# Preparing the DeltaNet chunks of a hybrid diffusion layer: loads, convolution, beta and the copies' engine

## The chip, the cores and the metric

The kernel runs on one core of a Trainium2 chip. The metric is the time of one execution on the device in microseconds (us). A core has five engines with an instruction queue each: TensorE (PE, with its weight loads as PEld) for matrix products, VectorE (DVE), ScalarE (ACT), GpSimd (POOL), and SyncE (SP), which here issues most of the transfers (DMAs). Matrix products write to PSUM, of which this kernel uses banks of 128 x 512 floats; everything else works on SBUF tiles of 128 partitions. Tensors that are too large for SBUF go through DRAM.

## The reference, cut to what matters

One layer works on 1024 latent tokens and 256 context tokens of width 1024. A modulated, RMS-normalised input is projected once; one half of the columns feeds a gated DeltaNet (4 heads of 128), the other a 2-D neighbourhood attention (8 heads of 64). Both are concatenated, projected, added to the input, and a SwiGLU feed-forward layer follows. The part that the change touches is the DeltaNet:

```python
qkv = short_conv(p[..., :3 * DN_WIDTH], conv_w)      # depthwise, 5 taps, centred, then SiLU
...
gam = cumsum(g)                                       # within a chunk
decay = exp(where(tril, gam[..., :, None] - gam[..., None, :], -inf))
kb = k * beta[..., None]
m = where(strict, einsum("bhncd,bhnmd->bhncm", kb, k) * decay, 0.0)
a_mat = eye(CHUNK) + m
u = triangular_solve(a_mat, v * beta[..., None], ...)
w = triangular_solve(a_mat, kb * exp(gam)[..., None], ...)
qk = where(tril, einsum("bhncd,bhnmd->bhncm", q, k) * decay, 0.0)
```

Both directions (forward, and backward over the flipped sequence) are scanned, the context first. The chunk's length does not alter the result, and the kernel uses chunks of 128.

## The kernel before, in words

**Stages.** (1) Norms, modulation and the first two blocks of the projection. (2) The rest of the projection as a list of `jobs` (lines 953 to 962), with the chunks' preparation beside it. (3) The scans over the chunks, with the neighbourhood attention beside them. (4) The output projection, and the feed-forward layer. The change lies in stage 2.

**Jobs.** A `Block` computes 128 output columns for all tokens, transposed: for each of eight slices of the input width, products of the high and low parts of weights and input (`mm_part`, line 390; matmuls at line 395). Kinds q, k and v are convolved along the tokens, nq and nk are the attention's. A `Wide` job computes 256 or 264 columns with the tokens on the partitions, tile by tile of 128 tokens (`wide`, line 573; matmuls at line 578): z, the output gate, goes to `z_d`, and nv, the attention's values, to `nv_d`. Each tile is copied from PSUM by ScalarE into `zt` (two buffers) and stored by a DMA that ScalarE's queue issues (lines 589 and 604). Weights pass a raw buffer of which there is one; ScalarE makes the high part (lines 197 and 570), GpSimd the low part (lines 198 and 571).

**A block's end.** `evac` copies the block from PSUM to `cr` (line 443) and issues all of the convolution to VectorE at once: a multiplication (line 447) and four multiply-adds (line 451), each in a context and a latent part. `silu` (line 458) follows on ScalarE at the end of the same job. `norm` is run in the next job, and `finish` in the one after: it makes the transposed copies and the products k k^T (`kk_d`) and q k^T (`qk_d`). After the second nv job, sixteen DMAs copy windows of `nv_d` into `vw_d` (line 1024). The main loop (lines 975 to 1028) takes a step of the background after each slice or tile: one to five generator steps.

**The background.** `block_inverses` solves the 32 x 32 diagonal blocks of `a_mat` for all 40 chunk-heads and both directions on VectorE (lines 824 and 826). The results `U` and their transposes `ut` (line 844) go to `x_d` (lines 845 and 846). `preps` then prepares 20 chunks: two directions times two context and eight latent chunks. The latent ones start when all q blocks are finished. At most three chunks are live, each takes one step in a round, and one further chunk may be loaded (`landing`, line 936).

**One chunk (`prep`, line 879).** `fetch` loads `kk` (k k^T, four heads), `xc` (the inverses of its blocks, both ways) and, for latent chunks, `at` (q k^T). Step 1: GpSimd multiplies the high and low parts of the log decays with a triangular mask into `rg` (line 886, 128 x 512 twice); ScalarE copies four diagonal blocks into `fx` (line 891), GpSimd four into `x0` (line 892). Step 2: TensorE sums the log decays (lines 896 and 897), ScalarE takes the exponential `e` (line 900), VectorE forms kk = kk * (-beta) * e, head by head since -beta differs (line 902; `NB` is minus beta over the squared norm of k), and am = at * e (line 906). Step 3: TensorE multiplies kk with fx (line 911), ScalarE copies the result (line 913). Steps 4 to 6: three products with the running sum, each followed by an addition on VectorE (lines 920 and 921). `y` is stored to `y_d`, `am` to `at_d`, by SP (line 930).

**What sets the order.** Every engine has one queue, worked off in order. The order within a queue is made when the program is built: a planner takes the instructions by priority, which is the program's order, as they become ready by its own cost estimates. So an instruction can stand ahead of one that was written before it; the sixteen copies of line 1024 stand between loads of the preparation on SP. A tile with n buffers can be written again when the tile n before it has been read. All DMAs share eight semaphores (100, 102 to 108 in the trace) in rotation, and a queue that issues one waits until the transfer that had the semaphore before has landed, whoever issued it.

Of the kernel before, what the change touches and what calls it, by code (L numbers as in the profile page):

```python
# [87 lines left out]
def hybrid(ctx, tc, a, dbg):  # L88
# [278 lines left out]
    with ExitStack() as bs:  # L367
# [30 lines left out]
        class Block:  # L398


            def __init__(self, kind, i):
                self.kind, self.i = kind, i
                self.segs = SEGS[1:] if kind in ("q", "nq") else SEGS
                self.t0 = self.segs[0][0]
# [16 lines left out]
            def evac(self):  # L421
# [22 lines left out]
                for lo, hi in ((0, CT), (CT, T)):  # L444
                    if hi <= t0:
                        continue
                    dve.tensor_scalar(acc[:, lo:hi], raw[:, lo:hi], cw[:, blk, 2:3], None, op0=OP.mult)
                    for tap in (0, 1, 3, 4):
                        o = tap - 2
                        d0, d1 = max(lo, lo - o), min(hi, hi - o)  # L450
                        dve.scalar_tensor_tensor(acc[:, d0:d1], raw[:, d0 + o:d1 + o],  # L451
                                                 cw[:, blk, tap:tap + 1], acc[:, d0:d1],
                                                 op0=OP.mult, op1=OP.add)

# [99 lines left out]
        class Wide:  # L554
# [27 lines left out]
            def tiles(self):  # L582
                half = self.half
                if self.kind == "nv":
                    for t in range(NCH):
                        p = self.wide(t, 0, 256)
                        vt = cp.tile([128, 264], F32, name="zt", tag="zt", bufs=2)
                        act.copy(vt[:, :256], p[:, :256])
                        act.dma_start(nv_d[t * 128:(t + 1) * 128, half * 256:half * 256 + 256], vt[:, :256])
                        yield  # L590
                    return
# [6 lines left out]
                for t in range(2, NCH):  # L598
                    p = self.wide(t, 0, 264)
                    zt = cp.tile([128, 264], F32, name="zt", tag="zt", bufs=2)  # L600
# [3 lines left out]
                    act.dma_start(z_d[(t - 2) * 128:(t - 1) * 128, half * 264:half * 264 + nz], zt[:, :nz])  # L604
                    yield

# [157 lines left out]
        def block_inverses():  # L764
            with ExitStack() as gs:
# [75 lines left out]
                for d in range(2):  # L841
                    ud = U[:, d * NU:(d + 1) * NU]
                    ut = g4.tile([128, NU, 32], F32, name="ut", tag="ut")
                    dve.transpose(fl(ut), fl(ud))
                    sp.dma_start(x_d[:, d, d], ud)
# [7 lines left out]
        def preps():  # L853

            first_half.close()
            with ExitStack() as gs:
# [11 lines left out]
                def fetch(d, c):  # L868

                    kk, xc = work("kk", 4), pp.tile([128, 2, 4, 32], F32, name="xc", tag="xc", bufs=2)  # L870
# [3 lines left out]
                    if c >= 2:  # L874
                        at = work("at", 2)
                        sp.dma_start(at, qk_d[:, c - 2])
                    return d, c, kk, xc, at

                def prep(n, d, c, kk, xc, at):
                    lat = c >= 2  # L880
                    mle = M[C_LE + d].rearrange("p (o i) -> p o i", o=1).to_broadcast([128, 4, 128])
                    rgs = []
                    for gg in (GH, GL):
                        rg = work("rg", 2, F32R)
                        src = gg.bitcast(F32)[:, d, c].rearrange("p (h o) -> p h o", o=1).to_broadcast([128, 4, 128])
                        pool.tensor_tensor(rg, src, mle, OP.mult)
                        rgs.append(rg)
                    x0, fx = x0s[n % 3], fxs[n % 2]
                    for b in range(4):
                        q = slice(b * 32, b * 32 + 32)  # L890
                        act.copy(fx[q, :, q], xc[q, 1])
                        pool.tensor_copy(x0[q, :, q], xc[q, 0])
# [6 lines left out]
                    e = work("y", 4)  # L899
                    act.activation(fl(e), p, AF.Exp)  # L900
                    for h in range(4):
                        dve.scalar_tensor_tensor(kk[:, h], kk[:, h], NB[:, d, c, h:h + 1], e[:, h],
                                                 op0=OP.mult, op1=OP.mult)
# [31 lines left out]
                while live or todo or landing:  # L935
                    if not landing and todo and (todo[0][1] < 2 or all(x in done for x in queries)):
# [38 lines left out]
        for n in range(2, len(jobs) + 2):  # L975
# [17 lines left out]
            nrm = blk(n - 1)  # L993
            if isinstance(j, Wide):
                for t, _ in enumerate(j.tiles()):
                    next(fin, 0)
                    if t == 4 and nrm:
                        nrm.norm()
# [10 lines left out]
            elif j:  # L1009
                for k in range(KT):  # L1010
                    j.mm([k])
                    if k >= 3:
                        next(fin, 0)
# [11 lines left out]
            if nrm:  # L1025
                nrm.norm()
            if isinstance(j, Block):
# [645 lines left out]
```

## Time and profile before

| | |
|---|---|
| median of 3 runs | 1618.23 us (1617.94 to 1624.84) |
| profiled execution | 1618.78 us, its span 1617.0 us |
| TensorE busy | 1512.7 us (94%) |
| VectorE, ScalarE, GpSimd busy | 1039.2, 706.2, 210.8 us |
| granted TensorE clock over the span | 0.979 |

The span runs from the first to the last instruction of the program. In the profile's lines, L911 is line 911; `out<-in` names the tiles; "x8" counts instructions; ACTq and SPq are an engine's queue issuing a DMA or waiting. A wait is idle time of an engine before an instruction, put down to whatever ended last before it. `issue` means that the profile shows nothing that was waited for. Stage 2 ends about 640 us into the span; the chunks' preparation runs from about 296 to 602 us, the four context chunks until about 337 us and the latent ones from 423 us on.

### The profile page before, as it was taken

Reading aid. Unit: us, or ns where it says so; the run is one execution under the profiler, and the core shown is the slowest. Engines: PE = TensorE matmul, PEld = TensorE weight load, DVE = VectorE, ACT = ScalarE, POOL = GpSimd, SP = SyncE. Lnnn points to the kernel's source line nnn. Section 1 sums busy time; section 2 is a strip of 40 time slices with the busy share of each in tenths; the row PEclk is TensorE's granted clock in tenths of the full one; section 3 lists DMA queues with packets and bytes.
Section 4 is the critical chain, followed back from the end, with each engine's and each line's share of the span. In section 5 each row is a group of like instructions: output and inputs, shape, how many; then the busy total and the mean of one; then the engine's idle time right before and its main releaser. Section 6 shows DMA issues by size and latency. Waiting matters only on the chain.

```text
span 1617.0 us, 24090 instructions
## 1 busy us (share of the span) xinstructions
PE 1512.7 (94%) x8642; PEld 1275.1 (79%) x8642; DVE 1039.2 (64%) x1931; ACT 706.2 (44%) x1341; POOL 210.8 (13%) x279
## 2 busy tenths in 40 slices
PE   2899899999989798999898999999999999999999
PEld 1689787778888786888787787888888888888887
DVE  4785678445264467577898638966656656679652
ACT  5353363663332234666674337433333333444441
POOL 0144611422232320111110000000000000000000
PEclk9898999999999899999999999999999999999999
DMA  9267121545346528999853910532223333698742
GB/s 370 89 209 218 56 76 40 177 129 173 120 126 194 185 95 212 312 282 283 234 178 119 324 46 33 196 105 98 98 98 110 101 109 113 231 365 307 253 157 85
DMA packets 206407, 271.03 MB, mean 168 GB/s; under 512 B 15952, under 2 KB 115792, under 8 KB 205264
## 3 DMA queue, kind: packets, MB, share of 16 engines
q1 hardware_dynamic: 200240, 264.14, 50.2%
q10 hardware_dynamic: 6048, 5.35, 1.0%
q8 instruction: 68, 1.11, 0.3%
q14 instruction: 51, 0.42, 0.1%
HBM read 204.68 MB, written 68.94 MB: 169 GB/s over the span
## 4 chain that ended last, share of the span: by engine, by line
PE 76%; DVE 10%; ACT 5%; DMA 4%; issue 2%; POOL 1%; SPq 0%; ACTq 0%; DVEq 0%; POOLq 0%
PE ps L1249 26%; PE ps L1592 13%; PE blk L395 11%; PE blk L578 4%; PE pr L920 3%; PE ps L1376 3%; PE sc L316 2%; PE sc L306 2%; PE sc L294 2%; DVE N L826 1%; DMA at<-qk_d 1%; DMA wad<-wa 1%; DVE tt L824 1%; DVE cacc L451 1%; PE pr L911 1%
## 5 line engine op out<-in xcount | busy, mean ns | idle before, releaser
L395 PE MATMUL blk<-hh,whi 128*128 128x512 f32 (+1 forms) x416 | 123.9, 390 | 1.4 <-ACT hh L690 1.0
L1310 ACT CAST uhi<-wq 128x512 fp32r<-128x512 f32 x101 | 60.4, 621 | 140.7 <-issue 61.6
L395 PE MATMUL blk<-hl,whi 128*128 128x512 f32 (+1 forms) x416 | 117.1, 374 | 5.0 <-DVE hl L692 5.0
L1310 ACT CAST uhi<-ws 128x512 fp32r<-128x512 f32 x91 | 54.7, 622 | 152.9 <-PE ps L1249 74.2
L395 PE MATMUL blk<-hh,wlo 128*128 128x512 f32 (+1 forms) x416 | 117.7, 375 | 0.6 <-POOL wlo L198 0.6
L1311 DVE TENSOR_TENSOR ulo<-wq,uhi 128x512 fp32r<-128x512 f32 x101 | 67.1, 686 | 69.0 <-ACT uhi L1310 38.9
L1249 PE MATMUL ps<-hT,uhi 128*128 128x512 f32 x336 | 104.0, 391 | 3.1 <-ACT hT L1424 3.1
L1249 PE MATMUL ps<-hT,ulo 128*128 128x512 f32 x336 | 103.9, 390 | 0.0
L1249 PE MATMUL ps<-lT,uhi 128*128 128x512 f32 x336 | 103.9, 391 | 0.0
L578 PE MATMUL blk<-zhi,hh 128*128 128x256 f32 (+2 forms) x304 | 90.1, 296 | 0.0
L1249 PE MATMUL ps<-hB,uhi 128*128 128x512 f32 x288 | 89.3, 391 | 0.0
L1249 PE MATMUL ps<-lB,uhi 128*128 128x512 f32 x288 | 89.2, 391 | 0.0
L395 PEld LDWEIGHTS blk<-hl,whi 128*128 128x128 f32 x416 | 73.7, 192 | 19.6 <-DVE hl L692 5.3
L1249 PE MATMUL ps<-hB,ulo 128*128 128x512 f32 x288 | 89.1, 390 | 0.0
L578 PE MATMUL blk<-zhi,hl 128*128 128x256 f32 (+2 forms) x304 | 88.4, 291 | 0.0
L578 PE MATMUL blk<-zlo,hh 128*128 128x256 f32 (+2 forms) x304 | 87.7, 289 | 0.0
L395 PEld LDWEIGHTS blk<-hh,wlo 128*128 128x128 f32 x416 | 73.3, 191 | 16.0 <-issue 1.6
L1311 DVE TENSOR_TENSOR ulo<-ws,uhi 128x512 fp32r<-128x512 f32 x91 | 60.7, 685 | 37.8 <-ACT uhi L1310 29.4
L395 PEld LDWEIGHTS blk<-hh,whi 128*128 128x128 f32 x416 | 71.3, 193 | 15.2 <-issue 3.6
L1249 PEld LDWEIGHTS ps<-hT,uhi 128*128 128x128 f32 x336 | 63.1, 189 | 16.5 <-ACT hT L1424 3.5
L1249 PEld LDWEIGHTS ps<-lT,uhi 128*128 128x128 f32 x336 | 63.4, 189 | 13.3
L1249 PEld LDWEIGHTS ps<-hT,ulo 128*128 128x128 f32 x336 | 63.3, 189 | 13.2
(341 smaller groups left out, 3719.5 us busy)
## 6 DMA issues: line engine op xcount, KB each, us to landing
wq<-w_fo SPq DMA_DIRECT2D x99, 256.0 KB
wq<-w_gu SPq DMA_DIRECT2D x88, 256.0 KB
wad<-wa SPq DMA_DIRECT2D x64, 256.0 KB
bt<-rpb SPq DMA_DIRECT2D x64, 192.0 KB
t_d<-g SPq DMA_DIRECT2D x22, 512.0 KB
fr<-t_d SPq DMA_DIRECT2D x44, 256.0 KB
f_d<-g SPq DMA_DIRECT2D x33, 256.0 KB
fr<-f_d SPq DMA_DIRECT2D x33, 256.0 KB
```

The source lines that it names most:

```text
L294: pe.matmul(sc[:, u * 640 + n0:u * 640 + n1], q, ks[i], start=i == 0, stop=i == 1)
L306: pe.transpose(sc[:, u * 640 + j * 128:u * 640 + (j + 1) * 128], bt[:, j * 128:(j + 1) * 128], ident)
L316: pe.matmul(sc[u * ND:u * ND + ND, 1280:1408], vv, pt[:, j * 128:(j + 1) * 128], start=j == 0, stop=j == 4)
L395: pe.matmul(o, ww[:, k], xx[k][:, s], start=k == 0 and j == 0, stop=k == KT - 1 and j == 2)
L451: dve.scalar_tensor_tensor(acc[:, d0:d1], raw[:, d0 + o:d1 + o], cw[:, blk, tap:tap + 1], acc[:, d0:d1], op0=OP.mult, op1=OP.add)
L578: pe.matmul(p[:, :c1 - c0], x[k][:, s], ww[:, k, c0:c1], start=k == 0 and j == 0, stop=k == KT - 1 and j == 2)
L920: pe.matmul(p[:, hs[h]], f[:, h], src[:, h], start=True, stop=True)
L1249: pe.matmul(o, w[wi][:, k], x[xi][:, k], start=first and k == 0 and j == 0, stop=k == n - 1 and j == 2, skip_group_check=True)
L1310: act.copy(hi, self.raw[key])
L1311: dve.tensor_tensor(lo, self.raw[key], hi.bitcast(F32), OP.subtract)
L1376: pe.matmul(o, w[wi][:, k], parts[xi][k][:, s], start=k == 0 and j == 0, stop=k == KT - 1 and j == 2)
L1592: pe.matmul(o[b], w[wi][:, b], F[xn, p][xi], start=n in (0, 1, 5) and p == 0 and j == 0, stop=p == NFB // 2 - 1 and j == 2, skip_group_che ...
```

## The change

Six edits in stage 2:

- A block's convolution becomes a generator: the multiplication, then one tap at a time for both parts. The next job takes one step of it per slice or tile. `silu` runs at its end, and not at the end of the block's own job.
- The DMAs that store nv and z tiles are issued by SP, one tile later (`held`); `zt` has three buffers.
- Minus beta is multiplied into the inverses that go to `fx`, once per direction, before they are stored in `x_d`. In a chunk, the four products of line 902 become one.
- Up to two chunks may be loaded ahead; `kk` has five buffers in place of four, `xc` and `at` three in place of two.
- `rg` is made by ScalarE, eight instructions of 128 x 128 in place of two of 128 x 512 on GpSimd, in four buffers in place of two. `x0` is filled by ScalarE too.
- `y` has five buffers in place of four.

```diff
@@ Block
-                for lo, hi in ((0, CT), (CT, T)):
-                    if hi <= t0:
-                        continue
+                self.taps = self.conv(raw, blk)
+
+            def conv(self, raw, blk):
+
+                acc = self.acc
+                parts = [(lo, hi) for lo, hi in ((0, CT), (CT, T)) if hi > self.t0]
+                for lo, hi in parts:
                     dve.tensor_scalar(acc[:, lo:hi], raw[:, lo:hi], cw[:, blk, 2:3], None, op0=OP.mult)
-                    for tap in (0, 1, 3, 4):
-                        o = tap - 2
+                yield
+                for tap in (0, 1, 3, 4):
+                    o = tap - 2
+                    for lo, hi in parts:
                         d0, d1 = max(lo, lo - o), min(hi, hi - o)
                         dve.scalar_tensor_tensor(acc[:, d0:d1], raw[:, d0 + o:d1 + o],
                                                  cw[:, blk, tap:tap + 1], acc[:, d0:d1],
                                                  op0=OP.mult, op1=OP.add)
+                    yield
+                self.silu()
@@ Wide.tiles (nv; z alike)
                         p = self.wide(t, 0, 256)
-                        vt = cp.tile([128, 264], F32, name="zt", tag="zt", bufs=2)
+                        if held:
+                            sp.dma_start(*held.pop())
+                        vt = cp.tile([128, 264], F32, name="zt", tag="zt", bufs=3)
                         act.copy(vt[:, :256], p[:, :256])
-                        act.dma_start(nv_d[t * 128:(t + 1) * 128, half * 256:half * 256 + 256], vt[:, :256])
+                        held.append((nv_d[t * 128:(t + 1) * 128, half * 256:half * 256 + 256], vt[:, :256]))
                         yield
+                    sp.dma_start(*held.pop())
@@ block_inverses
                     dve.transpose(fl(ut), fl(ud))
+                    x = (ut, ud)[d]
+                    dve.tensor_tensor(x, x, NB[:, d].rearrange("p c (h o) -> p (c h) o", o=1).to_broadcast(
+                        [128, NU, 32]), OP.mult)
                     sp.dma_start(x_d[:, d, d], ud)
                     sp.dma_start(x_d[:, d, 1 - d], ut)
@@ preps
-                    kk, xc = work("kk", 4), pp.tile([128, 2, 4, 32], F32, name="xc", tag="xc", bufs=2)
+                    kk, xc = work("kk", 5), pp.tile([128, 2, 4, 32], F32, name="xc", tag="xc", bufs=3)
...
-                        at = work("at", 2)
+                        at = work("at", 3)
...
-                    mle = M[C_LE + d].rearrange("p (o i) -> p o i", o=1).to_broadcast([128, 4, 128])
                     for gg in (GH, GL):
-                        rg = work("rg", 2, F32R)
-                        src = gg.bitcast(F32)[:, d, c].rearrange("p (h o) -> p h o", o=1).to_broadcast([128, 4, 128])
-                        pool.tensor_tensor(rg, src, mle, OP.mult)
+                        rg = work("rg", 4, F32R)
+                        for h in range(4):
+                            act.activation(rg[:, h], M[C_LE + d], AF.Copy, scale=gg.bitcast(F32)[:, d, c, h:h + 1])
...
                         act.copy(fx[q, :, q], xc[q, 1])
-                        pool.tensor_copy(x0[q, :, q], xc[q, 0])
+                        act.copy(x0[q, :, q], xc[q, 0])
...
-                    e = work("y", 4)
+                    e = work("y", 5)
                     act.activation(fl(e), p, AF.Exp)
-                    for h in range(4):
-                        dve.scalar_tensor_tensor(kk[:, h], kk[:, h], NB[:, d, c, h:h + 1], e[:, h],
-                                                 op0=OP.mult, op1=OP.mult)
+                    dve.tensor_tensor(kk, kk, e, OP.mult)
...
-                    if not landing and todo and (todo[0][1] < 2 or all(x in done for x in queries)):
+                    while len(landing) < 2 and todo and (todo[0][1] < 2 or all(x in done for x in queries)):
                         landing.append(fetch(*todo.pop(0)))
@@ main loop
+            taps = nrm.taps if nrm and nrm.taps else iter(())
             if isinstance(j, Wide):
                 for t, _ in enumerate(j.tiles()):
                     next(fin, 0)
+                    next(taps, 0)
                     if t == 4 and nrm:
+                        for _ in taps:
+                            pass
                         nrm.norm()
...
             elif j:
                 for k in range(KT):
                     j.mm([k])
+                    next(taps, 0)
...
             if nrm:
+                for _ in taps:
+                    pass
                 nrm.norm()
-            if isinstance(j, Block):
+            if isinstance(j, Block) and not j.taps:
                 j.silu()
```

More of the change, by code (lines that the diff above doesn't have):

```diff
@@ L402, in __init__ @@
                 self.kind, self.i = kind, i
+                self.taps = None
                 self.segs = SEGS[1:] if kind in ("q", "nq") else SEGS
@@ L583, in tiles @@
                 half = self.half
+                held = []
                 if self.kind == "nv":
@@ L599, in tiles @@
                     p = self.wide(t, 0, 264)
-                    zt = cp.tile([128, 264], F32, name="zt", tag="zt", bufs=2)
+                    if held:
+                        sp.dma_start(*held.pop())
+                    zt = cp.tile([128, 264], F32, name="zt", tag="zt", bufs=3)
                     act.activation(zt[:, :nz], p[:, :nz], AF.Silu)
@@ L603, in tiles @@
                         act.copy(ab[:, t], p[:, 248:264])
-                    act.dma_start(z_d[(t - 2) * 128:(t - 1) * 128, half * 264:half * 264 + nz], zt[:, :nz])
+                    held.append((z_d[(t - 2) * 128:(t - 1) * 128, half * 264:half * 264 + nz], zt[:, :nz]))
                     yield
+                sp.dma_start(*held.pop())
         first = [Block("k", 0), Block("k", 1)]
```

## The prediction

> **What bounds the kernel now.** I read the page first, then the stages in windows, then who ended TensorE's waits inside them, and last the chain and the single queues around each long wait.
>
> ```profile
> span 1617.0 us, 24090 instructions
> PE 1512.7 (94%) x8642; PEld 1275.1 (79%) x8642; DVE 1039.2 (64%) x1931; ACT 706.2 (44%) x1341; POOL 210.8 (13%) x279
> ```
>
> TensorE is busy 94%, and the change removes no matmul. So only its idle time, and the time it runs at a lowered clock, can be won. The windows (stretch, its length, busy time of PE, PEld, DVE, ACT and POOL, granted clock, DMA share, GB/s) cover the chunks' preparation:
>
> ```profile
> 285.00:345.00 60.00, 55.53 (x278) 43.74 (x277) 27.39 (x38) 36.85 (x62) 27.09 (x45) 0.97 0.47 153
> 345.00:425.00 80.00, 79.69 (x510) 71.63 (x509) 34.25 (x41) 32.38 (x46) 13.16 (x5) 0.98 0.46 148
> 425.00:520.00 95.00, 84.26 (x588) 77.56 (x587) 53.44 (x82) 33.50 (x73) 37.54 (x54) 0.95 0.49 152
> 520.00:608.00 88.00, 78.64 (x488) 69.40 (x487) 46.91 (x73) 24.93 (x49) 24.75 (x38) 0.94 0.45 146
> ```
>
> The first holds the four context chunks, the last two the sixteen latent ones. Idle in these two: 95 - 84.26 + 88 - 78.64 = 20.1 us. Lost to the clock: 0.05 x 95 + 0.06 x 88 = 10.0 us. The first adds 4.5 us idle and 0.03 x 60 = 1.8 us of clock. The ceiling of the whole change is the sum, 36.4 us, or 2.2%. The 80 us of the q blocks hold 0.3 us idle: nothing to win there. Who ended TensorE's waits, in 425 to 608 us and (second fence) 285 to 345 us (total, times, longest):
>
> ```profile
> PE pr L911 <- DVE y L921: 6.2, 3, 4.3
> PE pr L911 <- issue: 5.2, 2, 3.1
> PE pr L920 <- ACT kk L913: 4.3, 2, 3.1
> PE pr L911 <- DVE kk L902: 3.5, 6, 0.9
> ```
>
> ```profile
> PE pr L896 <- POOL rg L886: 2.0, 3, 1.3
> PE pr L911 <- DVE kk L902: 1.1, 2, 0.6
> ```
>
> The five longest, in TensorE's timeline (start, length, what, and in brackets the idle time before it):
>
> ```profile
> 449.08 1.16 PE L911 MATMUL pr<-fx,kk 128*128 128x128 f32 x8 [1.65 <-DVE y L921]
> ...
> 468.01 1.60 PE L911 MATMUL pr<-fx,kk 128*128 128x128 f32 x8 [2.07 <-issue]
> ...
> 506.53 2.07 PE L920 MATMUL pr<-y,kk 128*128 128x128 f32 x8 [3.11 <-ACT kk L913]
> ...
> 530.74 2.04 PE L911 MATMUL pr<-fx,kk 128*128 128x128 f32 x8 [3.12 <-issue]
> ...
> 547.54 2.07 PE L911 MATMUL pr<-fx,kk 128*128 128x128 f32 x8 [4.33 <-DVE y L921]
> ```
>
> The eight small matmuls behind the last three take about 2.05 us where those at 449 took 1.16: the lowered clock follows the wait. What stood behind 506 (chain of waits: start, length) and 530 (ScalarE's timeline), and, last line, behind 547:
>
> ```profile
> 491.70 4.25 DMA nv_d<-zt
> ...
> 497.51 7.88 DMA at<-qk_d
> ...
> 505.47 0.33 ACTq L589
> ...
> 505.89 0.59 ACT kk L913
> ```
>
> ```profile
> 525.36 0.33 ACTq L589 DMA_DIRECT2D nv_d<-zt  x1
> ...
> 528.42 0.33 ACTq L589 DMA_DIRECT2D nv_d<-zt  x1
> 528.79 0.60 ACT L900 ACTIVATE y<-pr 128x512 f32<-128x512 f32 x1 [2.64 <-DMA y_d<-y]
> ```
>
> ```profile
> 533.90 12.21 DMA at<-qk_d
> ```
>
> Twice ScalarE's queue stood at its own store of a value tile (L589), which could be issued only when an unrelated transfer had landed (at<-qk_d, y_d<-y); the copy and the exponential that TensorE needed were queued behind it. The third time a load of `at` took 12.21 us and the product with it (L906) held up VectorE.
>
> **The change, part by part.**
>
> *Stores leave ScalarE's queue.* The 20 nv and 16 z stores go to SP, one tile later. Gained: 3.11 + 3.12 = 6.2 us. Bounds: nothing, if the same waits come back on SP in front of the loads, and 6.2. I take 6.2, since SP's queue holds no evacuation. What SP pays, and what the loads behind it suffer:
>
> ```profile
> SPq L876 <- DVE am L906: 18.6, 6, 5.8
> SPq L1024 <- DMA nv_d<-zt: 11.7, 3, 5.3
> ```
>
> SP already waits 11.7 us for these very stores before the copies into vw_d (L1024); that wait stays. Each store takes 0.33 us of issue, as on ScalarE. What is queued behind a held store on SP: the loads of kk, xc and `at` for the next chunks, the stores of y and of the products with `at`, and the weights of the next job. The evacuation that a held store waits for is a whole tile old when it is issued, so only SP's rotation of landed transfers can hold it, as it held ScalarE. vw_d moves later by about one tile, and its readers belong to the attention stage, which the code starts after the last preparation. The z stores pass SP among the loads of the modulation's weights, in jobs ahead of these windows, where I count nothing for them or against them. Cost 0; the cover is the earlier loads, and without them the 4.33 us at 547 would stay.
>
> *Loads two ahead.* A third slot for `at` and `xc` and a fifth for `kk` lets SP issue a load without the 18.6 us it now stands waiting for L906 to free a slot. A chunk lasts 183 / 16 = 11.4 us; one chunk earlier covers most of a 12.21 us load. Gain 4.3 us, bounds 0 and 4.3.
>
> *Beta folded.*
>
> ```profile
> L902 DVE SCALAR_TENSOR_TENSOR kk<-kk,NB,y 128x128 f32<-128x128 f32 x64 | 31.4, 546 | 46.5 <-ACT y L900 46.5
> L906 DVE TENSOR_TENSOR am<-at,y 128x512 f32<-128x512 f32 x16 | 11.0, 688 | 3.9 <-DMA at<-qk_d 3.9
> L198 POOL TENSOR_TENSOR wlo<-wraw,whi 128x1024 fp32r<-128x1024 f32 x4 | 9.7, 2420 | 24.3 <-ACT whi L197 24.3
> ```
>
> ```profile
> L902 DVE SCALAR_TENSOR_TENSOR kk<-kk,NB,y x80: 335/344/2452, 305.6 to 593.5; 128x128 f32<-128x128 f32 x80
> ```
>
> The four products of a chunk take 31.4 / 16 = 1.96 us; one of the shape of L906 takes 0.69. So a chunk's chain shortens by 1.27 us. The kk waits are 0.9 us at most each, so all 3.5 us go; the 1.65 us at 449 are put down to y, and though the products stand ahead of y I count none of them. Bounds 0 and 3.5 + 1.65 = 5.2, taken 3.5. L902 takes 335 ns at best and up to 2452; I read the long ones as GpSimd working beside it. By the Trainium skill (SBUF — State Buffer, Who interferes with whom) VectorE with two SBUF inputs and GpSimd exclude each other for a whole instruction. The spread from 335 to 2452 agrees; by that rule L198 can still hold the new product for 2.42 us in four places, and the gain here would be 3.5 less some 2 us.
>
> The price is two multiplications of 128x1280 ahead of the stores of the inverses. The nearest rows:
>
> ```profile
> L802 DVE TENSOR_TENSOR W<-W,NB x1: 3582/3582/3582, 195.9 to 195.9; 128x1280 f32<-128x1280 f32 x1
> ...
> L804 DVE TENSOR_TENSOR W<-W,cst x1: 1491/1491/1491, 199.5 to 199.5; 128x1280 f32<-128x1280 f32 x1
> ```
>
> That is 3 to 7 us of VectorE for both. The store of an inverse waits for its product, and behind that store on SP stand the first loads of kk and xc, for which the first preparation waits; TensorE has block matmuls meanwhile. On the path 0 to 3.6 us. GpSimd being quieter then, I am nearer to the small row: 1 us.
>
> *A tap at a time.* The convolution's instructions stay, but others may come between them. At 468:
>
> ```profile
> 464.00 3.64 DVE L451 SCALAR_TENSOR_TENSOR cacc<-cr,cw,cacc 128x254 f32<-128x254 f32 x2
> 467.57 1.13 DVE L902 SCALAR_TENSOR_TENSOR kk<-kk,NB,y 128x128 f32<-128x128 f32 x4
> ```
>
> Two taps stood in front of the products. Bounds 0 and the 2.07 us; I take 1. The SiLU comes later by some block steps, and its reader, the block's transposes, a whole job later.
>
> *GpSimd's copies on ScalarE.*
>
> ```profile
> L1163 ACT ACTIVATE sq<-oacc x32: 292/297/313, 777.2 to 877.3; 128x128 f32<-128x128 f32 x32
> ```
>
> ```profile
> L891 ACT COPY fx<-xc 32x128 f32<-32x128 f32 x56 | 16.5, 295 | 1.2 <-issue 0.2
> ```
>
> ```profile
> L886 POOL TENSOR_TENSOR rg<-GH,cst 128x512 fp32r<-128x512 f32 x15 | 15.7, 1046 | 31.9 <-PE pr L896 31.7
> L892 POOL COPY x<-xc 32x128 f32<-32x128 f32 x52 | 15.8, 304 | 59.1 <-DVE y L921 45.9 <-DMA xc<-x_d 11.5
> ```
>
> Per chunk ScalarE gets 8 x 0.297 + 4 x 0.295 = 3.6 us, against 2 x 1.05 + 4 x 0.30 = 3.3 on GpSimd. Over sixteen chunks its busy share rises from (33.50 + 24.93) / 183 = 32% to (58.4 + 57.6) / 183 = 63%. There is room, but every one of these instructions can stand before an exponential or a copy that TensorE waits for. Bounds: 0, and a third of each burst, 16 x 1.2 = 19 us; with four slots for rg the bursts can run early, so 2 us. With the context chunks ScalarE rises from 36.85 to 36.85 + 14.4 = 51.3 of 60 us: bounds -2.0 (GpSimd's waits gone) and +8, taken +2. The Trainium skill (ScalarE: Activation LUTs, Rules for kernel authors) speaks against this part: it wants multiplications on VectorE and budgets about 0.3 us per instruction plus 0.83 ns per element. By it a burst would be 12 x 0.41 = 4.9 us, and the two costs of 2 us would be 5.4 us together, the sum 1.4 us worse; L1163 shows 0.297 us instead.
>
> *The clock.* 6.2 + 4.3 + 3.5 + 1 = 15.0 of 20.1 us idle go. The same share of 10.0 us of clock is 7.5; the small gaps that stay can lower the clock too, so 6 (bounds 0 and 10).
>
> *Sum.* -15.0 - 6 + 2 + 2 + 1 = -16.0 us. The profiled execution took 1618.78 us (the span plus 1.8), 0.55 above the median of the runs: 1618.2 - 16.0 = 1602.2, so **1602 us**.
>
> **The rivals.**
>
> *The waits move to SP (1613 us): the change doesn't do what it says.* The loads are two ahead in the code only: SP runs in order, and behind a store or a vw_d copy that waits, the load of `at` is as late as now. Then the 4.3 us stay, and half of the 6.2 and of the clock return: 3.1 + 3.5 + 1 + 3 - 5 = 5.6 won, 1612.6. For it: 11.7 us of SP's waits are for these stores. Against: the loads' own slot waits, 18.6 us, are the larger.
>
> *Everything clears (1586 us).* All idle and clock of the two windows go, 30 us, and the context stage gains its 2. For it: every long wait there has one of the edited causes. Against: 20.1 - 15.0 = 5.1 us of the idle time is many small waits for which I can name no edited cause, and each of them can lower the clock.
>
> *ScalarE becomes the bound (1631 us).* The place is its queue in 425 to 608 us.
>
> ```profile
> POOL x L892 <- DVE y L921: 45.9, 10, 10.8
> ```
>
> GpSimd stood 45.9 us at the x0 copies until an older chunk's last y was done, which cost nothing there. On ScalarE the same wait holds up whatever is behind it: the other chunks' exponentials and copies and the blocks' evacuations. With half a burst, 1.8 us, exposed per chunk: 16 x 1.8 = 29 us less the 16 won, +13. It decides from 16 / 16 = 1 us per chunk on. Against: 37% of ScalarE would still be free, and three slots of x0 leave it a round of the other chunks.
>
> **How the numbers follow.** Forecast 0.50 (own range 1594 to 1611), SP 0.20, all clears 0.12, ScalarE 0.18. A difference of 0.5%, 8.1 us, is about what a measurement of this kernel can tell from none. Below 1610: 0.9 of the forecast, 0.3 of SP and all of the third, 0.63. Above 1626: 0.8 of ScalarE and a little of SP, 0.15. Between: 0.22. From 1586 to 1628 leaves out about half of the third case (0.06) and 0.6 of the last (0.11).
>
> **What would show it.** Stores: no DMA issue on ScalarE in these windows, and the waits at L911 and L920 behind ScalarE under 2 us. Loads: no L906 waiting for at<-qk_d. Beta: one product of about 0.69 us per chunk. Taps: y or kk between them, no 2 us wait at the change of jobs. ScalarE: busy about 116 us in the two windows. Clock: 0.97 or more in them. Wrong would be a TensorE wait of over a microsecond per chunk on ScalarE, or the two windows together not shorter by 10 us.

## The result, and the profile after

The changed kernel takes 1609.59 us (median of 7 runs, 1608.93 to 1614.29), the kernel before 1619.36 us beside it (7 runs, 1617.94 to 1627.83). The ratio is 0.993, with a 95% interval of 0.9908 to 0.9952: faster by 9.8 us, where 16.0 were forecast. The profiled executions differ by less, 1617.0 to 1610.1 us of span. The page of the kernel after:

```profile
span 1610.1 us, 24094 instructions
PE 1508.0 (94%) x8642; PEld 1272.1 (79%) x8642; DVE 1015.4 (63%) x1873; ACT 771.8 (48%) x1581; POOL 143.8 (9%) x159
```

The same windows as before (stretch, length, busy time of PE, PEld, DVE, ACT and POOL, granted clock, DMA share, GB/s):

```profile
285.00:345.00 60.00, 53.78 (x271) 42.95 (x270) 23.42 (x26) 55.05 (x129) 8.05 (x7) 0.94 0.53 165
345.00:425.00 80.00, 79.53 (x509) 71.05 (x509) 35.69 (x43) 35.76 (x60) 12.27 (x5) 1.00 0.45 145
425.00:520.00 95.00, 89.48 (x656) 83.52 (x655) 42.03 (x58) 64.54 (x183) 9.76 (x4) 0.96 0.51 158
520.00:608.00 88.00, 77.06 (x484) 67.18 (x483) 43.13 (x58) 41.95 (x107) 5.91 (x6) 0.96 0.48 151
```

TensorE's idle time in 425 to 520 us falls from 10.7 to 5.5 us. In 520 to 608 it rises from 9.4 to 10.9, and in the context chunks from 4.5 to 6.2. Windows at fixed times hold different work in the two kernels, so here is one row each from the first matmul of the preparation to the last block matmul, before and after:

```profile
302.50:630.80 328.30, 304.46 (x1909) 268.99 (x1910) 173.27 (x254) 117.88 (x220) 96.76 (x135) 0.96 0.48 150
```

```profile
303.70:623.60 319.90, 298.14 (x1914) 264.57 (x1915) 145.49 (x194) 185.11 (x458) 31.29 (x19) 0.97 0.51 156
```

This stage is 8.4 us shorter. Only 2.1 us of that is idle time (23.8 to 21.8); 6.3 us is shorter busy time for the same matmuls. The clock explains some 3.5 of it (0.04 x 328.3 = 13.1 us lost before, 0.03 x 319.9 = 9.6 after; two digits make that rough). The rest of the span gives 1.5 us back: the stage starts 1.2 us later, and what follows takes 0.3 longer.

So TensorE waits nearly as long as before, but elsewhere. Who ended its waits in 425 to 608 us (total, times, longest) and in 285 to 345 us:

```profile
PE pr L936 <- ACT y L918: 7.2, 2, 7.0
PE pr L927 <- DVE kk L919: 5.2, 5, 2.3
PE pr L936 <- ACT kk L929: 3.0, 3, 2.0
```

```profile
PE pr L927 <- DVE kk L919: 3.5, 2, 2.6
PE pr L914 <- ACT rg L904: 1.4, 1, 1.4
```

The two waits behind ScalarE's own store (506 and 530 us before) and the one behind the late `at` (547) are gone. In their place stands one of 7.0 us. TensorE's timeline, and the chain of waits that leads there:

```profile
549.26 1.13 PE L927 MATMUL pr<-fx,kk 128*128 128x128 f32 x8 [2.34 <-DVE kk L919]
...
565.01 2.08 PE L936 MATMUL pr<-x,kk 128*128 128x128 f32 x8 [7.04 <-ACT y L918]
```

```profile
537.18 9.34 DMA xc<-x_d
...
553.21 9.79 DMA xc<-x_d
...
563.08 0.31 ACT fx L909
...
564.36 0.60 ACT y L918
```

Two loads of `xc`, the blocks of the inverses (128 KB each), take 9.3 and 9.8 us. ScalarE stands at its copies of them, and the exponential that TensorE needs is queued behind the copies. These loads were asked for among the sixteen copies into vw_d, which SP issues at about the same times as before (496.0 to 547.7 us there). The first two rows below are ScalarE's waits for the loads (x stands for x0, since numbers are left out); the last is the copies' line (shortest, median and longest issue in ns, first and last start):

```profile
ACT fx L909 <- DMA xc<-x_d: 7.2, 1, 7.2
ACT x L910 <- DMA xc<-x_d: 5.5, 1, 5.5
```

```profile
L1045 SPq DMA_DIRECT2D vw_d<-nv_d x16: 589/607/843, 492.8 to 549.7; - x16
```

### The profile page after: what moved, and what is told of

Its sections match the earlier page's. It is cut to its first block, busy times and chain, and to the rows that moved or that the text cites. A ratio compares the mean times of both kernels' runs of the same rounds, so it can differ in the third digit from the quotient of the medians.

```text
span 1610.1 us, 24094 instructions
## 1 busy us (share of the span) xinstructions
PE 1508.0 (94%) x8642; PEld 1272.1 (79%) x8642; DVE 1015.4 (63%) x1873; ACT 771.8 (48%) x1581; POOL 143.8 (9%) x159
## 4 chain that ended last, share of the span: by engine, by line
PE 75%; DVE 10%; ACT 7%; DMA 3%; issue 2%; POOL 1%; SPq 0%; ACTq 0%; DVEq 0%; POOLq 0%
PE ps L1272 26%; PE ps L1615 13%; PE blk L395 9%; PE blk L587 5%; PE ps L1399 3%; PE pr L936 2%; PE sc L316 2%; PE sc L306 2%; PE sc L294 2%; DVE N L842 1%; DMA xc<-x_d 1%; DVE tt L840 1%; PE ps L1148 1%; PE ps L1421 1%; PE ps L1139 1%
## 5 line engine op out<-in xcount | busy, mean ns | idle before, releaser
L198 POOL TENSOR_TENSOR wlo<-wraw,whi 128x1024 fp32r<-128x1024 f32 x18 | 44.3, 2459 | 349.3 <-ACT whi L197 310.2
```

Source lines behind the costliest of these rows:

```text
L198: lo_engine.tensor_tensor(o, r, h.bitcast(F32), OP.subtract)
```

## The experiments

Ratios are to the kernel before, with 95% intervals; those of the changed kernel are 0.993 [0.9908, 0.9952]. Differences under about 0.3% between two edits can't be told. A trace is one execution: that of the changed kernel took 2.3 us more than its median, that of the two-ahead loads alone 4.0 less. So traces are compared here by where the waits stand, and lengths that differ by a few us only roughly. The fifth buffer of y was not undone by itself.

**One edit undone at a time.** First the stores, back on ScalarE's queue:

```diff
-                        held.append((nv_d[...], vt[:, :256]))
+                        act.dma_start(nv_d[...], vt[:, :256])
-                        vt = cp.tile([128, 264], F32, name="zt", tag="zt", bufs=3)
+                        vt = cp.tile([128, 264], F32, name="zt", tag="zt", bufs=2)
```

> The changed kernel with one edit undone: the nv and z stores are issued by ScalarE again, at once, with two zt buffers. Theory (each removed wait was worth what the trace of before shows, and ScalarE's issue of the stores was the largest): the copies and exponentials queue behind the stores again, now with more of ScalarE's work behind them, and the kernel loses 5 to 9 us against the changed one: 1615 to 1619 us, with waits of 2 us or more behind ACTq in 425 to 608 us. Rival A (the stores were nothing; SP now pays the same): within 2 us of the changed kernel, 1608 to 1612 us.

1609.31 us, 0.9904 [0.9872, 0.9936]: nothing is lost. The waits behind ScalarE's store are back, with 4.3 us at 505, but the 7.0 us at 565 are gone. TensorE's waits in 425 to 608 us, then ScalarE's timeline at a store:

```profile
PE pr L929 <- ACT kk L922: 6.8, 4, 4.3
PE pr L920 <- DVE kk L912: 4.4, 3, 3.3
```

```profile
503.81 0.33 ACTq L598 DMA_DIRECT2D nv_d<-zt  x1
504.19 0.40 ACT L897 ACTIVATE rg<-cst,GL 128x128 fp32r<-128x128 f32 x1 [4.50 <-DMA vw_d<-nv_d]
```

ScalarE again stands 4.5 us in front of its own store until a transfer has landed, here a copy into vw_d. The edit removes that stall as the prediction said, and another of the same size takes its place. Next, the loads one chunk ahead, with the old buffers of kk, xc and at:

```diff
-                    while len(landing) < 2 and todo and (...):
+                    if not landing and todo and (...):
```

> The changed kernel with one edit undone: one chunk loaded ahead, kk, xc and at with four, two and two buffers. Theory (loads were late, and the wait of VectorE on at<-qk_d was one of them): 3 to 6 us slower than the changed kernel, 1613 to 1616 us, and a wait of am for at<-qk_d is back. Rival A (SP's order and the copies into vw_d, not the slots, set when a load lands): within 2 us of the changed kernel.

1618.18 us, 0.9969 [0.9949, 0.999]: 0.4% lost, some 6 us. It is the only edit whose undoing shows by itself, though its interval still touches that of the changed kernel. TensorE's waits, and below them ScalarE's and VectorE's:

```profile
PE pr L927 <- DVE kk L919: 12.5, 5, 7.0
```

```profile
ACT x L910 <- DMA xc<-x_d: 16.2, 2, 10.2
```

```profile
DVE am L922 <- DMA at<-qk_d: 5.2, 2, 4.7
```

The wait of am for `at` is back, as expected, and ScalarE's longest wait for `xc` is 10.2 us (7.2 in the changed kernel).

Third, `rg` and `x0` back on GpSimd:

```diff
-                        for h in range(4):
-                            act.activation(rg[:, h], M[C_LE + d], AF.Copy, scale=gg.bitcast(F32)[:, d, c, h:h + 1])
+                        pool.tensor_tensor(rg, src, mle, OP.mult)
-                        act.copy(x0[q, :, q], xc[q, 0])
+                        pool.tensor_copy(x0[q, :, q], xc[q, 0])
```

> The changed kernel with one edit undone: rg and x0 are made by GpSimd again, rg in two buffers; beta stays folded. Theory (the forecast's missing 6 us went to loads that are late beside the copies into vw_d, not to ScalarE's work): GpSimd's instructions hold up the one product on kk, 0.69 us becomes over 1, and the time is 1608 to 1613 us. Rival B (ScalarE's 3.6 us per chunk are what took the missing 6 us): 1602 to 1606 us, and the wait at the context chunks, 2.64 us before L927, is gone.

1614.52 us, 0.9937 [0.9914, 0.9959]: no difference. As expected, VectorE's product on kk is slower beside GpSimd, 1.43 us in the median where it took 0.69, but the time is not. The context chunks' 2.6 us wait for kk shrinks to 0.7, and GpSimd's `rg` costs 2.6 in its place (285 to 345 us):

```profile
PE pr L915 <- POOL rg L905: 2.6, 2, 2.3
PE pr L928 <- DVE kk L920: 0.7, 1, 0.7
```

The long wait stays, 6.7 us behind the exponential, since `fx` waits for the same `xc` on ScalarE as ever. `x0` alone on GpSimd (the last pair of the diff):

> The changed kernel with x0 filled by GpSimd again and rg still made by ScalarE. ScalarE stood 19.0 us for an older chunk's y and 5.5 us for xc at these copies. Theory (these stands are covered, as TensorE waits little for ScalarE outside the late loads): within 3 us of the changed kernel. Rival (the stands at x0 hold up exponentials and copies, and are where the forecast's 6 us went): 4 to 7 us faster than the changed kernel, 0.989 of the kernel before.

1611.22 us, 0.9939 [0.992, 0.9959]: no difference; the long wait is 8.8 us there. Beta per chunk again:

```diff
-                    dve.tensor_tensor(x, x, NB[:, d]..., OP.mult)
-                    dve.tensor_tensor(kk, kk, e, OP.mult)
+                    for h in range(4):
+                        dve.scalar_tensor_tensor(kk[:, h], kk[:, h], NB[:, d, c, h:h + 1], e[:, h],
+                                                 op0=OP.mult, op1=OP.mult)
```

> The changed kernel with one edit undone: minus beta is multiplied into kk in the chunk, head by head, and not into the stored inverses. With GpSimd nearly idle beside it, the four products should take 4 x 0.34 us and pipeline to about 1.1 us, against 0.75 us of the one product. Theory (the fold was worth its share of the kk waits only as long as GpSimd slowed the products): within 3 us of the changed kernel, whose ratio to the kernel before is 0.993; the start of the preparation 1 to 2 us earlier. Rival (the chunk's chain on VectorE is what TensorE waits for): 4 to 8 us slower than the changed kernel, waits on kk of 0.5 us or more at most chunks.

1610.1 us, 0.993 [0.9908, 0.9952]: nothing. The convolution in one piece again, as in the kernel before:

```diff
-                self.taps = self.conv(raw, blk)
+                for lo, hi in ((0, CT), (CT, T)):
+                    ...
```

> The changed kernel with one edit undone: a block's convolution is issued whole at the end of its own job, and SiLU there too. Theory (one wait of 2.1 us before, at the change from v0 to nv1): 1 to 4 us slower than the changed kernel; a wait of about 2 us for kk behind the taps is back near 468 us. Rival (the taps were nothing, since the planner already let other work between them): within 1 us.

1611.47 us, 0.9931 [0.9905, 0.9957]: nothing. In both, the long wait stands as before, 7.9 and 7.3 us.

**One edit alone.** The kernel before, with the two-ahead loads and their buffers and nothing else:

```diff
-                    kk, xc = work("kk", 4), pp.tile([128, 2, 4, 32], F32, name="xc", tag="xc", bufs=2)
+                    kk, xc = work("kk", 5), pp.tile([128, 2, 4, 32], F32, name="xc", tag="xc", bufs=3)
-                        at = work("at", 2)
+                        at = work("at", 3)
-                    if not landing and todo and (...):
+                    while len(landing) < 2 and todo and (...):
```

> The kernel before with one part of the change alone: loads two chunks ahead instead of one, with five, three and three buffers of kk, xc and at. Theory (the loads' distance is the part that carries the gain): undoing it in the changed kernel cost 0.4% (about 6 us), so alone it gives 5 to 8 us, ratio 0.995 to 0.997, and the waits behind ScalarE at 506.5 and 530.7 us (3.1 us each, its own DMA issues) stay, since the stores still stand on ScalarE. Rival (the parts only work together: with GpSimd's slow products and ScalarE's stores in place the loads wait for nothing that matters): ratio 0.998 to 1.000. Second rival (the loads alone carry all of it, the other six edits nothing): ratio 0.992 to 0.994.

1614.51 us, 0.996 [0.9941, 0.9979], as the first theory had it: alone the edit gives what its undoing costs. The waits behind ScalarE's own stores stay, though shorter than expected (1.9 and 2.5 us at most):

```profile
PE pr L911 <- issue: 4.6, 2, 2.5
PE pr L920 <- ACT kk L913: 3.4, 3, 1.9
```

That leaves about 0.3% for the other edits together, too little to be assigned to any of them (the two intervals overlap).

**The copies into vw_d.** Without them, attention reads its windows from nv_d itself, three loads of 64 KB in place of one of 192:

```diff
-            sp.dma_start(vw, vw_d[:, cb, half:half + 3, hp * 128:hp * 128 + 128])
+            for i in range(3):
+                sp.dma_start(vw[:, i], vlat[4 * (half + i):4 * (half + i) + 4, BLKS[cb]:BLKS[cb] + 32, hp * 128:hp * 128 + 128])
-                        sp.dma_start(vw_d[:, cb, ch], vlat[...])
```

> The changed kernel without the sixteen copies from nv_d into vw_d; the attention loads its value windows from nv_d itself, three transfers of 64 KB in place of one of 192 KB. Theory (the copies clog SP's queue and the DMA engines at 495 to 555 us, so that xc takes over 9 us and ScalarE stands for it): the 7.0 us wait at 565 and the 2.3 us one at 549 go, with the clock behind them 8 to 13 us faster than the changed kernel, 1597 to 1602 us, less what 64 more issues on SP cost in the attention (0 to 4 us). Rival B (ScalarE's work is the cause): within 3 us of the changed kernel, the two waits still there.

1613.71 us, 0.993 [0.9903, 0.9958]: the same time, but by other ways. Here are the preparation's and the attention's stage, and who ended TensorE's waits in 425 to 608 us:

```profile
302.00:609.40 307.40, 293.92 (x1914) 260.65 (x1913) 146.37 (x194) 184.13 (x457) 30.64 (x18) 0.99 0.47 146
609.40:864.30 254.90, 225.81 (x2012) 190.96 (x2010) 184.90 (x640) 160.15 (x407) 27.67 (x66) 0.95 0.79 233
```

```profile
PE pr L939 <- ACT kk L932: 3.1, 3, 2.1
PE pr L930 <- DVE kk L922: 3.1, 5, 1.6
```

The preparation loses all of its long waits and ends some 12 us shorter (307.4 against 319.9), at a clock of 0.99. So the copies are what makes the loads late. Attention gives 11.6 us back (254.9 against 243.3), where 0 to 4 were expected: TensorE there waits 15.3 us in all behind the scores' maximum (L299), 6.2 in the changed kernel. This run does not say whether the copies delay the loads by the bytes they move, by their place in SP's queue, or by the semaphores in rotation. The next one was to spread them, four after each of four jobs:

```diff
-            if isinstance(j, Wide) and n == values:
+            if values <= n < values + 4:
...
-                for cb in range(4):
+                cb = n - values
```

> The changed kernel with the sixteen copies from nv_d into vw_d issued four by four, at the end of nv1 and of the three v blocks after it, in place of all at the end of nv1. Same bytes, same attention. Without the copies the preparation ended 14 us earlier, and the attention with its 64 more transfers gave 12 us back. Theory (the copies' bunching at 495 to 555 us makes the loads of xc late): about half of the 14 us remain, 5 to 9 us faster than the changed kernel, 0.988 of the kernel before. Rival (the copies cost the same wherever they stand, since SP's queue and the DMA engines take them anyway): within 2 us of the changed kernel, other waits in place of those at 549 and 565.

1611.22 us, 0.9938 [0.9917, 0.9959]. It settles nothing: the planner put the copies where they had been.

```profile
L1045 SPq DMA_DIRECT2D vw_d<-nv_d x16: 594/602/898, 492.3 to 549.1; - x16
```

**Slack for what is late.** If the late `xc` is the missing gain, asking for it earlier should win it. The loads depend on nothing but the inverses, so they got a list of their own:

```diff
+                    while early and len(xcs) < 3:
+                        d, c = early.pop(0)
+                        xc = pp.tile([128, 2, 4, 32], F32, name="xc", tag="xc", bufs=4)
+                        sp.dma_start(xc, x_d[:, d, :, c * 4:c * 4 + 4])
+                        xcs.append(xc)
```

> The changed kernel, with each chunk's blocks of the inverses (xc, 128 KB from x_d) asked for three chunks before its kk and at, from six buffers instead of three; all else as it is. Theory (the rest of the forecast gain is lost in late xc loads): in the changed kernel's trace two xc loads take 9.3 and 9.8 us beside the copies into vw_d, ScalarE's copies fx and x0 stand 12.7 us for them in 425 to 608 us, and TensorE then waits 7.0 us at 565 and 2.3 us at 549. With the loads three chunks earlier those waits on xc are under 1 us in all, both TensorE waits go, the product matmuls end 6 to 10 us earlier, and the time is 1599 to 1604 us, some 0.4 to 0.6% below the changed kernel, ratio to the kernel before 0.987 to 0.990. Rival (the wait is only passed on: whatever is late beside the copies, TensorE loses the same): the waits on xc go, but waits of the same sum stand at another place between 500 and 608 us, behind kk or at loads or stores on the same queue; time within 2 us of the changed kernel's, 1608 to 1612 us, ratio 0.992 to 0.994.

The kernel that ran had four buffers of xc, not the six of that text. 1609.24 us, 0.9928 [0.9912, 0.9944]: the rival was right. No wait for `xc` is left on ScalarE. But the chain of waits has another late transfer, and TensorE waits 6.5 us:

```profile
549.09 10.22 DMA y_d<-y
...
559.39 0.61 ACT y L917
...
560.04 2.08 PE pr L935 x8
```

The exponential writes into a buffer of `y`, and that buffer is free only when the store of an older y has landed. So six buffers of xc, six of y, and three of rg to make room:

```diff
-                        rg = work("rg", 4, F32R)
+                        rg = work("rg", 3, F32R)
-                    e = work("y", 5)
+                    e = work("y", 6)
-                        xc = pp.tile([128, 2, 4, 32], F32, name="xc", tag="xc", bufs=4)
+                        xc = pp.tile([128, 2, 4, 32], F32, name="xc", tag="xc", bufs=6)
```

> The changed kernel with the blocks of the inverses asked for three chunks early from six buffers, and six buffers instead of five for y (the exponentials' output, whose buffer is free again when the store of an older y has landed); to make room, three buffers instead of four for rg. With the early blocks alone the waits of ScalarE for xc went, and the exponentials' own wait for a buffer of y came in their place: a store of y took 10.2 us beside the copies into vw_d, ScalarE stood 6.7 us for it, TensorE 6.5 us at 560. Theory (each transfer beside the copies is late by some 7 us, and a load or store that has one more chunk of slack is hidden): the 6.5 us wait goes too and nothing over 2.5 us stands between 425 and 608 us; time 1600 to 1606 us, ratio to the kernel before 0.988 to 0.991. Rival (it is passed on once more): a wait of 4 to 7 us stands in 540 to 580 us behind another transfer of the chunk (at, kk, the stores of at_d), time 1607 to 1612 us, ratio 0.992 to 0.994. Second rival: three buffers of rg now hold ScalarE, TensorE waits for rg at each chunk, 3 to 8 us in all.

1604.68 us, 0.9895 [0.9867, 0.9922]: the fastest kernel here by its time, and the preparation is 5.6 us shorter than the changed kernel's:

```profile
300.80:615.10 314.30, 296.82 (x1914) 263.90 (x1915) 146.38 (x194) 185.16 (x458) 32.15 (x19) 0.97 0.51 159
```

Its interval just overlaps that of the changed kernel, so "0.35% below" is likely and not sure; from the kernel with the stores on ScalarE and no slack (0.9904) it can't be told. The outcome lies between the theory and the rival: the time is the theory's, but a wait of 4.8 us came up behind a third transfer. The chain:

```profile
533.42 8.35 DMA nv_d<-zt
...
543.77 1.01 SPq L1055
...
544.89 10.99 DMA kk<-kk_d
...
555.97 1.29 DVE kk L918
...
559.55 2.07 PE pr L926 x8
```

SP stood until a value tile's store had landed, issued four copies (L1055), and the load of kk behind them took 10.99 us. The second rival fell: no wait for rg stands in 425 to 608 us. Last, the stores back on ScalarE together with this slack (xc two early from five buffers, six of y, four of rg):

> The changed kernel with three edits: the stores of nv_d and z_d back on ScalarE with two buffers of zt, the blocks of the inverses asked for two chunks early from five buffers, six buffers of y, and the four of rg. Theory: the late transfers beside the copies into vw_d are covered by the two edits of slack, and the stores on ScalarE, which cost nothing in the run that undid them alone (ratio 0.9904 to the kernel before), take transfers off SP's queue there; ScalarE still stands about 4 us at its own issues near 505 and 530. Time 1600 to 1606 us, ratio 0.988 to 0.991. Rival (the waits sum up to the same whatever edit is in): 1606 to 1612 us, ratio 0.9905 to 0.994, with the waits at 505 and 530 back (4.3 and 3.4 us) and no wait at 560. In both the same: if this one is not below the kernel with the stores on SP by more than 2 us, the stores' place is worth nothing with covered loads either.

1611.36 us, 0.9934 [0.9912, 0.9956]: the rival's numbers. It ran beside the kernel above, whose slowest run (1606.96 us) is below the fastest of this one (1607.45). Nothing waits at 560, but 4.3 us at 502 and 2.8 us at 527 stand behind ScalarE again:

```profile
PE pr L928 <- ACT kk L921: 7.0, 5, 4.3
PE pr L919 <- DVE kk L911: 3.9, 3, 2.8
```

Its preparation takes 319.2 us against 314.3. The two kernels differ by 6.7 us, but not in the stores' place alone: this one asks for xc two chunks early and not three, and has five buffers of xc and four of rg in place of six and three. That the stores' place is worth these us once the loads are covered fits the waits at 502 and 527 us, and is not shown; without that cover it was worth nothing.

## Why the prediction was right or wrong

The direction was right and the time lies in the range, 7.6 us above the forecast value. The likeliest case was not what happened in the trace, though. By the prediction's own marks it is partly wrong: ScalarE was to hold TensorE for less than 2 us at a time and held it for 7.0, and the preparation's stage is 8.4 us shorter, where the two windows together were to win at least 10. Part of the nearness is luck: the loads gave more than forecast, which hides that the stores and beta gave nothing that shows.

*Stores leave ScalarE's queue, -6.2.* The step that failed. Both waits went, as it said, and its lower bound was the truth: undoing the edit loses nothing. "Cost 0; the cover is the earlier loads" was the error, because the earlier loads did not cover. What came back was not a store that SP held up, but the loads beside the copies: in the chain of the changed kernel the second load of `xc` is issued behind a store of am, a copy into vw_d, loads of `at` and kk and a store of y (549.1 to 553.2 us), and then takes 9.8 us. The first rival, whose time (1613 us) was nearer than the forecast's, had that place right, SP's queue beside the copies, and the transfer wrong (`at`). In the runs with more slack the kernel with the stores on SP is 6.7 us faster, near the 6.2, but other buffers differ there too.

*Loads two ahead, -4.3.* Right in mechanism, too small: 0.4% in both directions, some 6 us. The step priced `at` alone. `xc` and `y` are on the same queue in the same 20 us, and one more chunk did not carry them across the copies. SP's own queue shows both halves: its wait for a slot of `at` falls from 18.6 to 7.3 us, the one for the nv stores ahead of the copies stays (11.7 before):

```profile
SPq L1045 <- DMA nv_d<-zt: 12.7, 4, 5.8
...
SPq L895 <- DVE am L922: 7.3, 4, 4.2
```

The row quoted for L892 already showed GpSimd standing 11.5 us for xc; the prediction priced only the 45.9 us beside it. ScalarE stood for the same load after the change, also where `x0` was given back to GpSimd.

*Beta, -3.5, its multiplications +1.* Each multiplication takes 1.49 us, as priced; what that costs on the path is not shown, since the preparation's first matmul starts anywhere from 300.6 to 306.1 us in the kernels that have this edit (302.5 before). The gain was not there. One product takes 0.69 us, as forecast (its line: shortest, median and longest in ns), but the waits on kk are 5.2 us in 425 to 608 us where they were 3.5, and only 2.6 us with beta per chunk again. Its line, and its group with the idle time before it:

```profile
L919 DVE TENSOR_TENSOR kk<-kk,y x20: 678/692/1675, 309.5 to 585.9; 128x512 f32<-128x512 f32 x20
```

```profile
L919 DVE TENSOR_TENSOR kk<-kk,y 128x512 f32<-128x512 f32 x16 | 12.0, 752 | 58.9 <-ACT y L918 48.3 <-DMA at_d<-am 10.5
```

VectorE stands 48.3 us for the exponential; a shorter product only starts that wait sooner. The waits put down to kk were ends of a chain whose late part lay elsewhere.

*A tap at a time, -1.* It gained nothing by itself. The program's order allows a product between any two taps, but the planner decides, and at one change of jobs four taps still stand in a row:

```profile
467.39 5.37 DVE L458 SCALAR_TENSOR_TENSOR cacc<-cr,cw,cacc 128x1022 f32<-128x1022 f32 x4
472.68 0.68 DVE L919 TENSOR_TENSOR kk<-kk,y 128x512 f32<-128x512 f32 x1
```

TensorE waits 1.58 us behind them at 473, where it waited 2.07 before.

*GpSimd's copies on ScalarE, +2 and +2.* Neither cost shows in the time, as undoing the edit gained nothing. In the context chunks idle time rises 1.75 us, but GpSimd's return only exchanges one wait for another. The clock of 0.94 there is not the copies' doing: in four runs with the same copies on ScalarE (stores, loads, beta or convolution undone) it is 0.97 to 1.00. ScalarE is busy 64.54 + 41.95 = 106.5 us in the two windows, not 116, chiefly because they hold the copies into rg of only 14 of the 16 chunks (2 x 56 of them, not 128). A scaled copy lasts 391 ns and not the 297 assumed, but in a row the next one starts before the last has ended, and four take 1.28 us:

```profile
L904 ACT ACTIVATE rg<-cst,GL 128x128 fp32r<-128x128 f32 x56 | 18.7, 391 | 0.0
```

```profile
553.01 1.28 ACT L904 ACTIVATE rg<-cst,GH 128x128 fp32r<-128x128 f32 x4
```

A burst is then 8 x 18.7 / 56 + 4 x 0.295 = 3.9 us, near the 3.6 of the prediction. The rule of the Trainium skill that the prediction set aside (ScalarE: Activation LUTs, Rules for kernel authors: about 0.3 us plus 0.83 ns per element) gives an estimate of 0.41 us for one of these instructions. The 391 ns of a single one agree with it; the 4.9 us that it gave for a burst do not come. The rival in which ScalarE becomes the bound did not come: it waits 19.0 us at `x0` for older chunks (45.9 on GpSimd), at no visible price. Nor did everything clear: even the kernel with more slack kept 17.5 us of idle time in its preparation (314.3 - 296.8).

*The clock, -6.* About 3.5 in the preparation's stage. It follows the waits: the eight matmuls behind the 7.0 us take 2.08 us, those at 549, behind 2.34 us, take 1.13. As the waits did not go, neither did the loss.

Of the prediction's signs, these came true: no DMA issue on ScalarE, no wait of the product with `at` for its load, one product of 0.69 us. The wait at the change of jobs fell below 2 us, to 1.58. These did not come true: waits behind ScalarE under 2 us, a clock of 0.97, ScalarE's 116 us.

## What to carry to other kernels

When a burst of large transfers shares a queue with the loads and stores of a pipeline, transfers that are issued among them can be late, and covering one can uncover the next: here xc, then y's store, then kk. Price all of them, or the burst itself, before crediting a single wait as gain. A wait is worth its length only if nothing else is late by as much at the same place; here moving the stores removed two waits of 3.1 us, and undoing the move cost nothing.

## What the runs showed of the hardware

Four transfers on the chains above, issued from 537 to 553 us in three kernels, took 9.3 to 11.0 us, whether they had 128 KB (xc) or 256 KB (y_d, kk). The chains pick out the late ones, so not every transfer took as long. The DMA engines' share (next to last number) in these 25 us, in the changed kernel and in the one without copies:

```profile
535.00:560.00 25.00, 20.62 (x133) 17.99 (x131) 7.10 (x11) 12.04 (x38) 0.00 (x0) 1.00 0.57 193
```

```profile
535.00:560.00 25.00, 24.68 (x158) 21.34 (x156) 12.52 (x19) 15.87 (x46) 2.37 (x1) 1.00 0.28 92
```

While the four were under way the share was higher, 0.60 and 0.76 for the loads of xc and 0.77 and 0.68 for y_d and kk, at 207 to 265 GB/s. So the bytes that were moved at the same time are not excluded as the cause. The Trainium skill (DMA: Bandwidth & Descriptors, Two DMAs through the same engine are not ordered) says that descriptors of one queue start in order on each DMA engine. By it a load issued behind four copies starts only after them; that 128 KB were hardly quicker than 256 KB agrees, but no run here put the copies on another queue, so it stays open.

The same 128 x 128 on ScalarE took 297 ns as a square of f32 and 391 ns as a scaled copy into fp32r, and in a row each further copy added some 0.30 us; what costs the 94 ns was not tried. And a product of two 128 x 512 tiles on VectorE took 0.69 us in the median with rg and x0 made by ScalarE, and 1.43 us with GpSimd making them beside it.
